# A two-layer hybrid backbone on one core: the scheduler's assumed delays between engines and for transfers raised, and its order and priorities chosen anew under them

## The chip, the cores and the metric

The kernel runs on one core of a Trainium2 chip. Time is device time in microseconds (us) of one execution, and the number that counts is the median of the runs: 2003.44 us of three (1996.93, 2003.58 and 2003.44). The core has TensorE for matmuls (PE, with its weight loads shown as PEld), VectorE (DVE), ScalarE (ACT), GpSimd (POOL) and SyncE (SP), which issues most transfers.

## What is computed

Two layers over 1024 latent tokens and 256 context tokens of width 1024. Each layer normalises and modulates its input, projects it once (34 tiles of 128 columns and 16 small gate columns), runs three groups of heads on the pieces, projects the concatenated outputs back and adds them to the stream through a gate. Cut to what matters:

```python
for l in range(DEPTH):                                   # 2 layers
    mod = jax.nn.silu(c) @ w_mod[l] + b_mod[l]           # shift, scale, gate; the same for the context
    h  = rms_norm(x, norm_g[l]) * (1.0 + scale) + shift
    hc = rms_norm(y, norm_g[l]) * (1.0 + scale_c) + shift_c
    pl, pc = split_cols(h @ w_in[l]), split_cols(hc @ w_in[l])
    a_l, a_c = attention_mixer(...)   # windowed attention, 8 heads, rotary, sink, context keys; * silu(z)
    g_l, g_c = gdn_mixer(...)         # gated DeltaNet, both directions: conv, l2norm, chunks of 128 here,
                                      # a triangular inverse per chunk, then a chain over the chunks
    r_l, r_c = lru_mixer(...)         # conv, block-diagonal gates, linear scan in both directions
    x = x + gate * (concat(a_l, g_l, r_l) @ w_out[l])
    y = y + gate_c * (concat(a_c, g_c, r_c) @ w_out[l])  # layer 0 only
return rms_norm(x, final_g)
```

## The kernel before

The kernel has no loop that fixes the order of its instructions. Each piece of work is a Python generator (a thread) that yields operations with an engine, a cost and the buffers that are read and written: `inproj` multiplies the input projection's tiles, `kq_thread`, `v_thread` and `lru_thread` do the convolutions and gates, `prep_thread` and `inv_thread` prepare the DeltaNet chunks, `gjob`, `gside` and `gchain` run them, `att_block`, `att_half` and `score_thread` do the attention, `stage3` splits the outputs (`osplit`) and multiplies the output projection, `mod_thread` makes the modulation vectors. Large products are done in three fp32r passes (high half times high half, high times low, low times high), which the rows show as `whi` and `wlo`.

While the program is built, `Driver.run` plays a list scheduler. It keeps a planned clock for every engine and every buffer; at each step it takes, of all threads that stand ready, the one with the lowest key, that is the planned start plus the thread's priority (`PR` for layer 0, `PR1` for layer 1) plus a few penalties, and issues its instruction. What it issues becomes the fixed order of the engine's queue on the chip; the planned times themselves reach the chip in no form. The delays that it assumes:

- `LATS` (line 22): what is added after the end of an operation on PE, ACT, DVE or POOL before another engine may use the result.
- the line `end = self.dma + ...` (line 394): what is added after a transfer's planned end, and `dmabw`, the bytes per microsecond that transfers share.
- `Driver.fill` (called in `run`): where PE's next operation would start later than PE is free by its plan, and it opens a fresh PSUM buffer, the scheduler issues dummy matmuls of the identity with itself (128x128 fp32, 0.226 us each by its plan) until 0.3 us before that start; a filler is put in only where at least two fit. In the orders below these are the rows `psum<-ident_114 128x128`. Before the first real products, `warm` issues more of the same kind. A filler is an instruction like any other: it runs whether PE had to wait there or not.

PE's order is thus work, and fillers where the plan has a hole. Lines that the steps below speak of: 595 is the helper that issues every matmul; 705 and 711 are ACT's copy and PE's transposes for the modulation; 741 and 747 the sums of squares before a norm; 1256 and 1263 take a projection's PSUM away; 1554 is the transfer that crosses two halves of the partitions for the LRU gates; 1728 to 1781 are the copies of a DeltaNet chunk's inverse; 1888 and 1894 finish DeltaNet; 1968, 1989, 2056, 2088 and 2090 are attention's maximum, exponential, transposes and their copies; 2023 transposes its denominators. The attention's keys and queries (`kstd`, `qstd`) are loaded through ACT's own DMA queue (`q_att = "aq"`), the rest through SP's.

Of the kernel before, what the change touches and what calls it, by code (L numbers as in the profile page):

```python
# [18 lines left out]
EPS = 1e-6  # L19
XSIZE, YSIZE = 21376, 21584  # L20
LAT = 0.2
LATS = dict(pe=0.2, act=0.14, dve=0.12, pool=0.08)
HOST = dict(gq="pool", aq="act")
BLK = {"A": (256, 512), "B": (768, 512), "C": (0, 256)}
SPANS = ((0, 512), (512, 512), (1024, 258))
# [208 lines left out]
class Driver:  # L234


    def __init__(self):
        self.eng = dict(pe=0.0, act=0.0, dve=0.0, pool=0.0, sp=0.0, aq=0.0, gq=0.0)
        self.dma = 0.0
        self.threads, self.blocked = [], []  # L240
        self.set, self.free = "", ("inproj", "oproj", "mod0")
        self.trace = None
        self.regions = []
        self.clock = Clock()
        self.PR = {"att": -2.23, "att_k": -6.13, "att_q": -24.94, "atth": 0.51, "ba": 1.24, "evac": -0.21,
                   "gchain": 0.84, "gdn_q": -4.1, "gdn_v": 0.22, "gfin": -5.94, "gprep": 0.61, "gside": 1.08,
                   "inproj": 1.35, "inv": 0.4, "lru_x": -0.17, "lru_z": -1.8, "modlate": -1.43, "modload":
                   -12.04, "norm": 0.21, "normA": -13.11, "normB": -12.92, "normC": -5.67, "nrmB": -2.77,
                   "nrmC": 0.25, "oproj": 0.39, "osplit": -1.28, "prep": -3.38, "ptev": -5.63, "resid": -0.56,
                   "rope": 1.5, "score": -0.16, "warm": 4.18, "wprep": -10.67, "z": -1.27}  # L250
        self.ops, self.late = [], False
        self.PR1 = {"att": -1.75, "att_k": -24.84, "att_q": -1.75, "atth": -0.51, "ba": 0.55, "evac": 0.23,
                    "gchain": 1.03, "gdn_q": -5.85, "gdn_v": 0.65, "gfin": 2.81, "gprep": -1.81, "gside": 0.09,
                    "inproj": 0.71, "inv": 0.22, "lru_x": -0.54, "lru_z": 1.01, "normA": -0.05, "normB": 2.27,
                    "normC": 13.57, "oproj": -0.41, "osplit": 0.31, "prep": -2.79, "ptev": -6.8, "resid":
                    -11.31, "rope": 6.72, "score": -2.09, "wprep": 0.18, "z": -1.15}
        self.margin, self.setpen, self.tilepen = 2.88, 1.24, 0.43
        self.cap = {"pe": 0.51, "dve": 0.34, "act": 0.28, "pool": 0.53}
        self.filler, self.fillmin = None, 2
        self.port, self.tile, self.sync, self.dry = dict(dve=0.0, pool=0.0), "", {}, False  # L260
        self.waitc, self.dmabw = dict(act=0.06, dve=0.05, pool=0.04, sp=0.047, gq=0.04), 300e3

    def spawn(self, gen, prio=0.0, name="", done=None):
        th = Thread()
# [40 lines left out]
    def ready(self, name, R, Wr):  # L305

        start = self.eng[name]
        lat = LATS.get(name, 0.0)
        for b in R:
# [17 lines left out]
    def run(self):  # L327
        while self.threads or self.blocked:
            self.settle()
            best = None  # L330
            for th in self.threads:
                _, cost, fn, R, Wr = th.op
                name, st = th.eng, th.st
                start = self.ready(name, R, Wr)
                p = th.prio

                if name in self.cap and start > self.eng[name] and p < -self.cap[name]:
                    p = -self.cap[name]
                key = start + p
                if name == "pe" and start > self.eng["pe"] and not th.free:  # L340
                    key += self.margin
                if name == "pe":
                    if st != self.tile:
                        key += self.tilepen
                elif st and st not in self.set.split(","):
                    key += self.setpen
                if best is None or key < best[0]:
                    best = (key, start, th)
            if best is None:
                if not self.blocked:  # L350
                    break
                raise RuntimeError("stuck: " + "; ".join(f"{t.name}:{t.op[0]}:{getattr(t.op[1], 'name', '')}" for t in self.blocked))
            _, start, th = best
            self.threads.remove(th)
            _, cost, fn, R, Wr = th.op
            name, st = th.eng, th.st
            if name == "pe":
                if self.filler:
                    self.fill(start, Wr)
                if st != self.tile:  # L360
                    start += 0.093
                    self.tile = st
            elif st and st not in self.set.split(","):
                start += 1.3
                self.set = {"t": "t,e", "l": "l,e", "s": "s", "e": "t,e"}[st]
                if st == "l":

                    self.table("natural_log_exp_and_others")
            if self.trace is not None:
                self.trace(th.name, name, start, cost, R, Wr)  # L370
            if not self.dry:
                fn()
            pre = set()
            k = len(self.ops)
            for b in R:
                pre.add(b.wo)
            for b in Wr:
                if not b.dram:
                    pre.add(b.wo)
                    pre.update(b.ro.values())  # L380

            seen = {}
            for i in pre:
                if 0 <= i < k and self.ops[i] != name and i > self.sync.get((name, self.ops[i]), -1):
                    seen[self.ops[i]] = max(i, seen.get(self.ops[i], -1))
            for e2, i in seen.items():
                self.sync[name, e2] = i
            start += self.waitc.get(name, 0.0) * max(0, len(seen) - 1)
            if name in ("sp", "aq", "gq"):
                self.eng[name] = start + (0.6 if name == "gq" else 0.42)  # L390
                if name in HOST:
                    self.eng[HOST[name]] = self.eng[name]
                self.dma = max(self.dma, start) + cost / self.dmabw
                end = self.dma + (4.5 if name == "gq" else 2.2)
            else:
                end = start + cost if name != "pe" else self.clock.run(start, cost, 0.5 if st else 1.0)
                self.eng[name] = end
                if name in ("dve", "pool") and not any(b.psum for b in R) and not any(b.psum for b in Wr):
                    self.port["pool" if name == "dve" else "dve"] = end
                end += LATS[name]  # L400
            for b in R:
                b.ro[name] = k
            for b in Wr:
                b.wo, b.ro = k, {}
            self.ops.append(name)
            for b in R:
                if end > b.r:
                    b.r, b.re = end, "" if name in ("sp", "gq") else name
            for b in Wr:
                b.virgin = False  # L410
                if end > b.w:
                    b.w, b.we = end, "" if name in ("sp", "gq") else name
            self.advance(th)
# [142 lines left out]
class Build:  # L556
# [467 lines left out]
    def params(self):  # L1024
# [37 lines left out]
        for k in "aeflr":  # L1062
            for l in range(2):
                yield ops[k, l]

    ORDER = ("gdn_k0", "gdn_q1", "gdn_v1", "gdn_k1", "gdn_q0", "gdn_k2", "gdn_q2", "lru_x3", "att_q0", "gdn_z3",
             "gdn_k3", "lru_x0", "lru_z3", "att_v0", "gdn_q3", "gdn_v3", "lru_z0", "lru_x2", "lru_x1", "lru_z2",
             "att_q2", "gdn_v0", "att_z2", "lru_z1", "gdn_z2", "gdn_v2", "att_q3", "att_q1", "att_k0", "gdn_z1",
             "gdn_z0", "att_z3", "att_z0", "att_z1")
    ORDER1 = ("gdn_q0", "lru_z2", "gdn_q1", "gdn_k0", "gdn_k1", "gdn_v3", "gdn_k2", "gdn_k3", "gdn_q2",  # L1070
              "gdn_v2", "gdn_q3", "lru_x3", "lru_z1", "lru_x1", "gdn_z0", "att_v0", "lru_z0", "lru_x2",
              "lru_z3", "att_z1", "gdn_v1", "att_q2", "gdn_v0", "lru_x0", "att_k0", "att_q0", "att_q3",
              "att_q1", "att_z0", "att_z2", "att_z3", "gdn_z2", "gdn_z3", "gdn_z1")

    def ev(self, *k):
        return self.events.setdefault(k, Event())
# [13 lines left out]
    def phase_a(self, l):  # L1090
# [10 lines left out]
        C["lock_lru"], C["lock_kq"], C["lock_att"], C["lock_inv"] = self.lock(1), self.lock(2), self.lock(2), self.lock(1)  # L1101
        order = self.order(l, self.ORDER1 if l else self.ORDER)
        jobs, boxes = self.wjobs(l, order)
# [1229 lines left out]
```

## Time and profile before

| | |
|---|---|
| median of the runs | 2003.44 us |
| the profiled execution's own time | 2003.42 us |
| its span, first to last instruction | 2001.7 us |
| PE busy | 1936.9 us, 97% |
| DVE, ACT, POOL busy | 1312.9, 1062.0, 424.1 us (66%, 53%, 21%) |
| mean granted clock of TensorE | 0.986 |
| moved by DMA | 338.04 MB, 169 GB/s over the span |

The profiled execution and the median agree within 0.02 us, so sums are made against either; 1.7 us lie outside the span. PE is busy nearly all the time, so what can be won or lost lies in three places: time in which PE waits, time in which its clock is granted at the lower of its two levels, and matmuls that compute nothing (the fillers). A profile's busy time of PE has the fillers in it. The program runs through these stretches: 0 to 110 us loads and first norms, 110 to 545 the input projection of layer 0 with convolutions and gates, 545 to 1000 DeltaNet, attention and the start of the output projection, 1000 to 1110 the turn to layer 1, 1110 to 1530 its input projection, 1530 to 1870 its DeltaNet and attention, then the last projection, and a tail of 11.7 us without matmuls.

### The profile page before, as it was taken

How to read it: one execution, taken by the hardware profiler on the slowest of the kernel's cores; microseconds unless marked ns; L12 is line 12 of the kernel's file. 1: busy time of each engine (PE TensorE's matmuls, PEld its weight loads, DVE VectorE, ACT ScalarE, POOL GpSimd, SP SyncE). 2: the span in 40 equal slices, each digit the busy share in tenths (PEclk: the TensorE clock that was granted, in tenths of full speed). 3: DMA queues.
4: the chain of work that ended last, by engine and by line, in shares of the span. 5: the costliest groups of instructions: out<-in, count | busy, mean ns of one | idle time of the engine just before them, and what ended most of it. 6: DMA issues, size and time to landing. Idle time of an engine off the chain costs nothing. (4 is left out here: it accounts for less than half of the span.)

```text
span 2001.7 us, 35422 instructions
## 1 busy us (share of the span) xinstructions
PE 1936.9 (97%) x13244; PEld 1560.5 (78%) x13244; DVE 1312.9 (66%) x2568; ACT 1062.0 (53%) x1897; POOL 424.1 (21%) x604
## 2 busy tenths in 40 slices
PE   8999999999999989999999999999999999999997
PEld 5688778888888966767788788877777888776786
DVE  5666699697844465774624668899788434787433
ACT  4467677565533254665523577676665322566432
POOL 2302100100055631001332111200001765100232
PEclk9999999999999999999999999999999999999998
DMA  8135633614588897655633156562444878544653
GB/s 301 35 108 172 180 110 95 182 54 137 182 280 266 263 299 239 201 163 148 225 106 119 45 170 177 156 166 64 137 142 173 284 224 258 162 133 124 200 169 105
DMA packets 311597, 338.04 MB, mean 169 GB/s; under 512 B 62993, under 2 KB 220289, under 8 KB 311425
## 3 DMA queue, kind: packets, MB, share of 16 engines
q1 hardware_dynamic: 290544, 321.05, 52.0%
q10 hardware_dynamic: 20880, 14.73, 2.4%
q8 instruction: 104, 1.70, 0.4%
q14 instruction: 69, 0.56, 0.1%
HBM read 235.58 MB, written 94.87 MB: 165 GB/s over the span
## 5 line engine op out<-in xcount | busy, mean ns | idle before, releaser
L595 PE MATMUL psum<-regx,whi 128*128 128x512 f32 (+1 forms) x3328 | 952.1, 372 | 8.5 <-ACT regy L1263 3.7
L595 PEld LDWEIGHTS psum<-regx,whi 128*128 128x128 f32 x3328 | 592.2, 189 | 125.8 <-issue 12.2
L595 PE MATMUL psum<-regx,wlo 128*128 128x512 f32 (+1 forms) x1664 | 609.8, 366 | 0.0
L595 PEld LDWEIGHTS psum<-regx,wlo 128*128 128x128 f32 x1664 | 314.6, 189 | 52.9 <-DVE wlo L876 0.2
L595 PE MATMUL psum<-regy,regy 128*128 128x128 f32 (+4 forms) x4064 | 318.7, 265 | 10.4 <-DMA regy<-regy 4.2
L595 PEld LDWEIGHTS psum<-regy,regy 128*128 128x128 f32 (+2 forms) x4064 | 266.1, 148 | 55.1 <-issue 26.9
L871 ACT ACTIVATE whi<-raw 128x1024 fp32r<-128x1024 f32 (+1 forms) x132 | 125.6, 952 | 167.7 <-PE psum L595 144.7
L595 PE MATMUL psum<-regx,regx 128*64 128x256 f32 (+2 forms) x1184 | 190.3, 363 | 4.7 <-DMA regx<-kstd 2.5
L595 PEld LDWEIGHTS psum<-regx,regx 128*64 128x64 f32 (+1 forms) x1184 | 112.9, 162 | 56.3 <-issue 25.9
L595 PE MATMUL psum<-regy,whi 128*128 128x512 f32 (+1 forms) x576 | 156.4, 359 | 0.1
L876 DVE TENSOR_TENSOR wlo<-raw,whi 128x1024 fp32r<-128x1024 f32 (+1 forms) x100 | 114.2, 1143 | 54.6 <-ACT whi L871 54.3
L876 POOL TENSOR_TENSOR wlo<-raw,whi 128x768 fp32r<-128x768 f32 x32 | 60.8, 1899 | 388.0 <-ACT whi L871 385.1
L1989 ACT ACTIVATE regx<-regx,regx 128x640 f32<-128x640 f32 (+2 forms) x144 | 109.0, 760 | 21.0 <-DVE regx L1981 11.9
L1356 DVE SCALAR_TENSOR_TENSOR regy<-regy,gcv,regy 128x1282 f32<-128x1282 f32 x72 | 111.9, 1556 | 9.3 <-ACT regy L1352 7.9
L595 PEld LDWEIGHTS psum<-regy,whi 128*128 128x128 f32 x576 | 101.4, 189 | 19.7 <-issue 4.2
L1263 ACT ACTIVATE regy<-psum 128x512 f32<-128x512 f32 (+1 forms) x124 | 65.2, 527 | 93.8 <-PE psum L595 87.4
L1669 POOL TENSOR_TENSOR regy<-regy,regy 128x512 f32<-128x512 f32 x76 | 96.8, 1295 | 75.9 <-DMA regy<-kqd 49.3
L1712 POOL TENSOR_SCALAR_AFFINE_SELECT regy<-regy 128x128 f32<-128x128 f32 (+1 forms) x240 | 68.8, 323 | 207.7 <-DMA regy<-Md 77.8
L2199 DVE SCALAR_TENSOR_TENSOR regy<-psum,modT,regy 128x512 f32<-128x512 f32 (+1 forms) x40 | 27.8, 696 | 126.9 <-PE psum L595 126.9
L2090 ACT ACTIVATE regx<-psum 128x512 f32<-128x512 f32 x114 | 65.2, 593 | 81.6 <-PE psum L2056 77.1
L595 PE MATMUL psum<-regy,wlo 128*128 128x512 f32 (+1 forms) x288 | 102.7, 357 | 0.3 <-POOL wlo L876 0.2
L2056 PE MATMUL psum<-ident,regx 128*128 128x128 f32 x640 | 94.0, 279 | 4.8 <-ACT regx L2090 1.9
(200 smaller groups left out, 2606.8 us busy)
## 6 DMA issues: line engine op xcount, KB each, us to landing
raw<-in_win_dram SPq DMA_DIRECT2D x68, 512.0 KB
raw<-in_wout_dram SPq DMA_DIRECT2D x64, 384.0 KB
regy<-kqd SPq DMA_DIRECT2D x76, 256.0 KB
raw<-in_wmod_dram SPq DMA_DIRECT2D x32, 512.0 KB
regy<-od SPq DMA_DIRECT2D x24, 512.0 KB
regy<-egd SPq DMA_DIRECT2D x40, 256.0 KB
regy<-ktd SPq DMA_DIRECT2D x40, 256.0 KB
regy<-vtd SPq DMA_DIRECT2D x40, 256.0 KB
```

What stands on the lines that cost most here:

```text
L595: self.nc.tensor.matmul(out, lhsT, rhs, start=start, stop=stop, skip_group_check=True)
L871: yield ("act", c_act(n), lambda: nc.scalar.activation(hi.t[:, :n], raw.t[:, :n], AF.Copy), [raw], [hi])
L876: (nc.gpsimd if e == "pool" else nc.vector).tensor_tensor(lo.t[:, :n], raw.t[:, :n], hi.t[:, :n].bitcast(F32), OP.subtract)
L1263: yield ("act", c_act(n), lambda: nc.scalar.activation(dst.t[:m, o:o + n], ps.t[:m, :n], AF.Copy), [ps], [dst])
L1356: yield ("dve", c_dve(GW), lambda: nc.vector.scalar_tensor_tensor(y.t[:, :GW], xp.t[:, k:k + GW], w[:, k:k + 1], y.t[:, :GW], OP.mult, OP. ...
L1669: yield ("pool", c_pool(512), lambda: nc.gpsimd.tensor_tensor(b.t, b.t, ga.t, OP.mult), [ga, b], [b])
L1712: nc.gpsimd.affine_select(out[:, :, 32 * b:32 * b + 32], src, [[0, 4], [0, 32]], OP.is_ge, 0.0, base=32 * b + 31 if up else -32 * b, chann ...
L1989: yield ("act:e", c_act(nk, 1) + .1, lambda: nc.scalar.activation(P, P, AF.Exp, bias=one(0, h), scale=-1.0, accum_out=one(8, h)), [Ps[j], ...
L2056: nc.tensor.transpose(pt.t[:, 128 * j:128 * j + 128], Ps[j].t[:, 128 * i:128 * i + 128], self.I.t)
L2090: yield ("act", c_act(512), lambda: nc.scalar.activation(PT.t, pt.t, AF.Copy), [pt], [PT])
L2199: yield ("dve", c_dve(n), lambda: nc.vector.scalar_tensor_tensor(xn.t[:, :n], ps.t[:, :n], g.t[:, 16 + dt, who:who + 1], xn.t[:, :n], OP.m ...
```

## The change

The assumed delays are raised, the transfers' bandwidth is lowered a little, all planned clocks start at 3 to 4 us instead of zero, and under these numbers priorities, tile orders, penalties and caps were chosen anew. No operation of the kernel's computation is added or removed; the order of nearly all of them moves, and the number of fillers with it.

```diff
-LATS = dict(pe=0.2, act=0.14, dve=0.12, pool=0.08)
+LATS = dict(pe=0.35, act=0.4, dve=0.4, pool=0.4)
...
-        self.eng = dict(pe=0.0, act=0.0, dve=0.0, pool=0.0, sp=0.0, aq=0.0, gq=0.0)
-        self.dma = 0.0
+        self.eng = dict(pe=4.0, act=4.0, dve=4.0, pool=4.0, sp=3.0, aq=4.0, gq=4.0)
+        self.dma = 4.0
...
-        self.PR = {"att": -2.23, "att_k": -6.13, "att_q": -24.94, "atth": 0.51, "ba": 1.24, "evac": -0.21,
+        self.PR = {"att": -2.03, "att_k": -10.38, "att_q": -23.44, "atth": 0.38, "ba": -2.37, "evac": 0.28,
...
-        self.margin, self.setpen, self.tilepen = 2.88, 1.24, 0.43
-        self.cap = {"pe": 0.51, "dve": 0.34, "act": 0.28, "pool": 0.53}
+        self.margin, self.setpen, self.tilepen = 2.91, 1.5, 0.43
+        self.cap = {"pe": 0.45, "dve": 0.35, "act": 0.03, "pool": 0.45}
...
-        self.waitc, self.dmabw = dict(act=0.06, dve=0.05, pool=0.04, sp=0.047, gq=0.04), 300e3
+        self.waitc, self.dmabw = dict(act=0.06, dve=0.05, pool=0.04, sp=0.047, gq=0.04), 285e3
...
-                end = self.dma + (4.5 if name == "gq" else 2.2)
+                end = self.dma + (5.0 if name == "gq" else 3.2)
...
-    ORDER = ("gdn_k0", "gdn_q1", "gdn_v1", "gdn_k1", "gdn_q0", "gdn_k2", "gdn_q2", "lru_x3", "att_q0", "gdn_z3",
+    ORDER = ("gdn_k2", "gdn_q1", "gdn_k0", "gdn_v3", "gdn_k1", "gdn_q0", "gdn_v0", "lru_x3", "att_q2", "gdn_z3",
...
```

Counted over PE's whole order, the matmuls go from 10335 to 10453, and all of the difference is fillers: 139 before, 257 now. Of these, 106 and 110 stand among the first loads and norms, before the input projection runs without a break; behind that there are 33 in 7 places before (2, 5, 2, 2, 9, 5, 8) and 147 in 21 places now (2, 19, 3, 4, 24, 3, 2, 3, 6, 15, 3, 11, 6, 4, 4, 7, 2, 7, 6, 3, 13). What stands around DeltaNet changes too. Of the 400 32x32 matmuls with which layer 0 starts its chunks' inverses, 360 stood ahead of attention's first transposes and 80 do now; in layer 1 it was all 400, now 160. Of the input projection, 264 matmuls stood between the first of these 32x32 rows and the end of attention in layer 0, and 24 do now (150 and 84 in layer 1).

Three places in PE's order. The first is the first late modulation chunk of layer 0, whose transposes (L711) need ACT's copy of a product of PE. Before, `regy` rows are DeltaNet, L1894 finishes two of its chunks:

```order
L1894 MATMUL psum_87<-ident_114,regy_4437 128x128 x4
L595 MATMUL psum_81<-regy_4413,regy_4419 64x64 x4
L595 MATMUL psum_85<-regy_4232,regy_4422 64x64 x4
L595 MATMUL psum_84<-ident_114 128x128 x2
L1894 MATMUL psum_84<-ident_114,regy_4438 128x128 x4
L595 MATMUL psum_82<-regy_4411,regy_4420 32x32 x8
L595 MATMUL psum_82<-regy_4414,regy_4425 32x32 x8
L711 MATMUL psum_86<-ident_114,regx_6082 128x128 x4
```

Now the same transposes stand behind attention's scores (`regx,regx`, 256 columns each), and two fillers:

```order
L595 MATMUL psum_82<-regx_4936,regx_4939 128x256
L595 MATMUL psum_82<-regx_4937,regx_4939 128x256
L595 MATMUL psum_82<-regx_4936,regx_4939 128x256
L595 MATMUL psum_82<-regx_4937,regx_4939 128x256
L595 MATMUL psum_87<-regx_4934,regx_4939 128x256
L595 MATMUL psum_87<-regx_4935,regx_4939 128x256
L595 MATMUL psum_86<-ident_114 128x128 x2
L711 MATMUL psum_86<-ident_114,regx_5051 128x128 x4
```

The small 32x32 products just ahead of the transposes are replaced by longer ones that depend on loads alone.

The second place is the end of attention in layer 0. Before, output projection rows (`regy,whi` and `regy,wlo`) stand between the last products with the values (64x256) and the last denominators (L2023):

```order
L595 MATMUL psum_84<-regx_6080,regx_6046 64x256 x2
L595 MATMUL psum_84<-regx_6077,regx_6046 64x256 x2
L595 MATMUL psum_83<-regx_6079,regx_6046 64x256 x2
L595 MATMUL psum_83<-regx_6076,regx_6046 64x256 x2
L595 MATMUL psum_81<-regy_7190,whi_172 128x512
L595 MATMUL psum_81<-regy_7183,whi_172 128x512
L595 MATMUL psum_81<-regy_7190,wlo_174 128x512
L595 MATMUL psum_81<-regy_7190,whi_172 128x512
L595 MATMUL psum_81<-regy_7183,whi_172 128x512
L595 MATMUL psum_81<-regy_7190,wlo_174 128x512
L2023 MATMUL psum_82<-ident_114,regx_6086 8x128
```

Now fillers stand there:

```order
L2056 MATMUL psum_80<-ident_114,regx_5034 128x128
L2056 MATMUL psum_80<-ident_114,regx_5035 128x128
L595 MATMUL psum_82<-regx_5046,regx_4938 64x256 x2
L595 MATMUL psum_82<-regx_5049,regx_4938 64x256 x2
L595 MATMUL psum_81<-ident_114 128x128 x24
L2023 MATMUL psum_81<-ident_114,regx_5056 8x128
L595 MATMUL psum_80<-ident_114 128x128 x3
L2056 MATMUL psum_80<-ident_114,regx_5037 128x128
```

The output projection of layer 0 no longer begins before the last attention block is transposed (90 of its matmuls stood ahead of that, none does now).

The third place is the end of PE's order: the last output projection, fillers, and the sum of squares of the final norm (`ones`). Before:

```order
L595 MATMUL psum_82<-regx_15910,whi_172 128x512
L595 MATMUL psum_82<-regx_15909,wlo_174 128x512
L595 MATMUL psum_86<-ident_114 128x128 x8
L595 MATMUL psum_86<-regy_15427,ones_119 128x512
```

Now:

```order
L595 MATMUL psum_84<-regx_16035,whi_172 128x512
L595 MATMUL psum_84<-regx_16034,wlo_174 128x512
L595 MATMUL psum_80<-ident_114 128x128 x13
L595 MATMUL psum_80<-regy_15516,ones_119 128x512
```

Five more fillers stand between the same two operations.

## Rows read from the trace of the kernel before

**Rows 1.** The page: busy time of each engine, share of the span, instructions

```profile
PE 1936.9 (97%) x13244; PEld 1560.5 (78%) x13244; DVE 1312.9 (66%) x2568; ACT 1062.0 (53%) x1897; POOL 424.1 (21%) x604
```

**Rows 2.** Stretches of the run: length, busy time (instructions) by engine, clock, DMA

```profile
core 0: us, PE busy (x) PEld busy (x) DVE busy (x) ACT busy (x) POOL busy (x), PEclk, DMA share, GB/s
0.00:110.00 110.00, 98.26 (x594) 70.79 (x595) 68.28 (x124) 52.65 (x93) 31.00 (x40) 0.97 0.45 153
110.00:1990.00 1880.00, 1838.65 (x12652) 1489.69 (x12650) 1238.17 (x2439) 1006.18 (x1800) 388.48 (x561) 0.99 0.56 170
1000.00:1110.00 110.00, 108.99 (x604) 90.34 (x602) 44.44 (x68) 31.86 (x51) 29.87 (x25) 1.00 0.32 105
1870.00:1990.00 120.00, 119.55 (x523) 96.68 (x521) 43.25 (x49) 40.46 (x53) 36.04 (x22) 1.00 0.51 156
```

**Rows 3.** PE's waits from 110 to 1990 us: total us, times, longest

```profile
PE psum L711 <- ACT regx L705: 4.4, 2, 2.3
PE psum L595 <- DMA regy<-regy: 4.2, 2, 3.4
PE psum L595 <- ACT regy L1263: 3.7, 3, 2.9
PE psum L595 <- POOL regy L1781: 3.0, 2, 2.5
...
PE psum L595 <- DMA regx<-kstd: 2.5, 2, 1.5
PE psum L595 <- DVE regx L1256: 2.3, 1, 2.3
PE psum L2056 <- ACT regx L2090: 1.9, 1, 1.9
PE psum L595 <- DVE regy L741: 1.7, 2, 1.2
PE psum L595 <- DVE regy L809: 1.5, 1, 1.5
PE psum L1894 <- DVE regx L2088: 1.4, 1, 1.4
...
PE psum L595 <- DMA regx<-qstd: 1.4, 1, 1.4
...
PE psum L1894 <- DVE regy L1888: 1.1, 1, 1.1
...
PE psum L595 <- DVE wlo L876: 0.2, 1, 0.2
```

**Rows 4.** Two of the seven stretches with the lower clock, columns as in rows 2

```profile
224.00:234.00 10.00, 8.02 (x34) 4.82 (x35) 5.67 (x13) 4.03 (x6) 0.21 (x2) 0.66 0.63 178
...
1706.00:1716.00 10.00, 8.94 (x57) 8.60 (x58) 6.41 (x24) 0.76 (x2) 3.50 (x3) 0.66 0.83 242
```

**Rows 5.** Timeline of PE: start, length, instructions, and the wait before them

```profile
29.04 7.53 PE L595 MATMUL psum<-ident 128*128 128x128 f32 x66
...
711.47 1.11 PE L711 MATMUL psum<-ident,regx 128*128 128x128 f32 x4 [2.34 <-ACT regx L705]
...
1718.29 2.61 PE L595 MATMUL psum<-regx,regx 128*128 128x256 f32 x16 [1.37 <-DMA regx<-qstd]
```

**Rows 6.** Timeline of ACT's queue: issues of the attention's loads

```profile
705.88 3.28 ACTq L600 DMA_DIRECT2D regx<-kstd  x4
...
1709.45 0.38 ACTq L600 DMA_DIRECT2D regx<-qstd  x1
```

**Rows 7.** Timeline of the end, DVE and PE

```profile
1986.50 1.95 PE L595 MATMUL psum<-ident 128*128 128x128 f32 x16
...
1988.15 0.69 DVE L741 TENSOR_TENSOR regy<-regy,regy 128x512 f32<-128x512 f32 x1 [0.69 <-ACT regy L747]
1988.89 1.13 PE L595 MATMUL psum<-regy,ones 128*128 128x512 f32 x2 [0.45 <-DVE regy L741]
```

More of the change, by code (lines that the diff above doesn't have):

```diff
@@ L244, in __init__ @@
         self.clock = Clock()
-        self.PR = {"att": -2.23, "att_k": -6.13, "att_q": -24.94, "atth": 0.51, "ba": 1.24, "evac": -0.21,
[L246 to L250, printed above, removed]
@@ L251, in __init__ @@
-        self.ops, self.late = [], False
[L252 to L256, printed above, removed]
@@ L257, in __init__ @@
-        self.margin, self.setpen, self.tilepen = 2.88, 1.24, 0.43
-        self.cap = {"pe": 0.51, "dve": 0.34, "act": 0.28, "pool": 0.53}
+        self.PR = {"att": -2.03, "att_k": -10.38, "att_q": -23.44, "atth": 0.38, "ba": -2.37, "evac": 0.28,
+                   "gchain": 0.14, "gdn_q": -7.53, "gdn_v": 1.15, "gfin": -2.6, "gprep": 0.05, "gside": 0.87,
+                   "inproj": 1.32, "inv": 0.3, "lru_x": -0.17, "lru_z": -1.78, "modlate": -1.51, "modload":
+                   -18.36, "norm": 0.86, "normA": -14.03, "normB": -20.5, "normC": -14.47, "nrmB": -4.95,
+                   "nrmC": 0.93, "oproj": -2.68, "osplit": -2.43, "prep": -4.88, "ptev": -2.64, "resid": 0.29,
+                   "rope": 3.63, "score": -0.16, "warm": 5.4, "wprep": -8.27, "z": -1.59}
@@ new lines, in __init__ @@
+        self.ops, self.late = [], False
+        self.PR1 = {"att": -2.89, "att_k": -27.69, "att_q": -0.58, "atth": -0.73, "ba": -3.03, "evac": 0.4,
+                    "gchain": -4.34, "gdn_q": -7.45, "gdn_v": 0.76, "gfin": 2.56, "gprep": -1.98, "gside": -0.5,
+                    "inproj": 0.76, "inv": 0.22, "lru_x": -0.54, "lru_z": -2.86, "normA": 0.93, "normB": 2.36,
+                    "normC": 8.47, "oproj": 0.35, "osplit": -0.41, "prep": -2.77, "ptev": -8.75, "resid": -8.03,
+                    "rope": 11.72, "score": -1.25, "wprep": -1.6, "z": -1.47}
@@ L1064, in params @@
                 yield ops[k, l]
-    ORDER = ("gdn_k0", "gdn_q1", "gdn_v1", "gdn_k1", "gdn_q0", "gdn_k2", "gdn_q2", "lru_x3", "att_q0", "gdn_z3",
[L1067 to L1073, printed above, removed]
+    ORDER = ("gdn_k2", "gdn_q1", "gdn_k0", "gdn_v3", "gdn_k1", "gdn_q0", "gdn_v0", "lru_x3", "att_q2", "gdn_z3",
+             "att_v0", "lru_x0", "lru_z3", "gdn_k3", "gdn_q2", "gdn_q3", "gdn_z0", "lru_z0", "att_z1", "gdn_v1",
+             "lru_z2", "lru_x2", "att_q3", "gdn_z1", "lru_z1", "gdn_v2", "att_q0", "att_k0", "lru_x1", "att_z2",
+             "att_z3", "att_q1", "att_z0", "gdn_z2")
+    ORDER1 = ("gdn_q0", "lru_z3", "gdn_q1", "gdn_k0", "gdn_k1", "gdn_v2", "gdn_k3", "gdn_k2", "gdn_q2",
+              "gdn_v3", "gdn_q3", "lru_x0", "lru_z2", "lru_x1", "gdn_z2", "lru_z1", "lru_z0", "lru_x3",
+              "att_v0", "att_z2", "gdn_v1", "gdn_v0", "lru_x2", "att_q0", "att_k0", "att_q1", "att_q2",
+              "att_q3", "gdn_z1", "gdn_z0", "att_z3", "gdn_z3", "att_z1", "att_z0")
     def ev(self, *k):
```

## The prediction

> **What bounds the kernel now.** I read the page first: PE is busy for 1936.9 of 2001.7 us and no other engine is near it, the next being DVE with 1312.9 [rows 1]. So the order of PE's queue is the time, and all that a new order can change is what PE does besides its work. The table of stretches gives this in three parts. Up to 110 us PE idles 110 - 98.26 = 11.7 us; there the first loads set the pace, and both orders issue the same loads first. From 110 to 1990 us it idles 1880 - 1838.65 = 41.35 us, and its granted clock is 0.99 there, so about 0.01 x 1880 = 18.8 us of full-speed time are lost at the lower level [rows 2]. Behind 1990 us lie 11.7 us in which the last norm runs on other engines.
>
> The list of PE's waits tells what the 41.35 us are: 41 waits in 27 rows, of which the twelve with waits over 1 us and the last are shown, and no large one. Thirteen waits are longer than 1 us: 2.3 and 2.1 for ACT's copy before L711, 3.4 for the LRU transfer, 2.9 for L1263, 2.5 for POOL, 2.3, 1.9, 1.5, 1.5, 1.4, 1.4, 1.2 and 1.1 [rows 3]; the 2.1 is what the first row's 4.4 leaves. They sum to 25.5 us, and the other 28 to 15.85. The lower clock follows the longer ones: seven times the granted clock falls to 1.2 GHz, each time around one of these waits. Two of the seven are shown, 34% of 10 us each, so 3.4 us lost each [rows 4]; two more lose as much and three some 1.7 us.
>
> The third part is not a wait. A filler costs what work costs: 66 records, two to a filler, take 7.53 us, so 33 fillers take 7.53 and one takes 0.228 us [rows 5]. The 33 late fillers of before are 7.5 us. So between 110 and 1990 us some 41.35 + 18.8 + 7.5 = 67.6 us are not work, and only these can move.
>
> **The change, part by part.** *Work.* Nothing is added or removed but fillers, so PE's products cost what they cost now.
>
> *Fillers.* Behind the first stretch they go from 33 to 147, that is 114 x 0.228 = 26.0 us more on the engine that sets the end. Nothing hides them. They are no loss where PE would have waited as long anyway, and a loss elsewhere; I count them in full and count waits apart. Ahead of 110 us they go from 106 to 110; PE waits there for loads, so the four are taken at nothing (0.9 us if the loads were early).
>
> *Waits that become shorter.* The plan now allows 0.35 to 0.4 us after an operation where it allowed 0.08 to 0.2, some 0.25 us more, and 1.0 us more after a transfer. The planned distance between an operation and the one that needs it thus grows by 1 us where one transfer or four operations lie between, which is about what most waits have behind them (a product of PE, an ACT or DVE copy, a second vector operation, PE again). Where there is no work to put in between there are fillers, and the wait is gone too. I therefore take 1 us from every wait. The 28 short ones vanish, 15.85 us; of the thirteen long ones 25.5 - 13 = 12.5 us stay. Bounds: none is shortened (0 us) and all vanish (41.35 us); I take the value between, since the places shown bear it out. At the first modulation transposes PE waited 2.34 us [rows 5] behind two rows of small 32x32 products; now six score products and two fillers stand ahead of them.
>
> *The clock.* It falls around waits that last; if thirteen long waits shrink to half (25.5 to 12.5), I take half of the 18.8 us as won back, 9.4. Bounds are 0 and 18.8, and fillers, which are products, speak for the upper half.
>
> *The places that lose.* At the end of the kernel 8 fillers and then 0.45 us of waiting covered the chain resid, square, add [rows 7]. Two more fillers would have been enough; five are added, 0.7 us too many. DVE's add ends at 1988.84 and PE starts at 1988.89 [rows 7], so a hand-over takes 0.05 us where the plan now has 0.4: the new delays are longer than the chip's. At the end of attention in layer 0, 24 + 3 fillers stand where the output projection stood, 6.2 us; PE's wait there before was 1.9 us, for L2090 [rows 3]. From 1000 to 1110 and from 1870 to 1990 us PE idled 1.0 and 0.45 us [rows 2], and 15 + 3 + 11 fillers now stand at the turn to layer 1, 3 + 6 between output tiles of layer 0 and 6 + 3 between those of layer 1. These are all in the 26.0 us.
>
> *DeltaNet beside attention.* Before, most chunks' inverses ran ahead of attention, with the input projection's tail between them; now most stand between attention's rows. It changes what waits on what, but the sum of work per engine is the same, and DVE and ACT are busy for 66% and 53% [rows 1]; I take it at nothing, with 10 us to either side for the range, about a quarter of the 41.35 us.
>
> *Sum.* 2003.4 + 26.0 - 15.85 - 13.0 - 9.4 = 1991.2 us against the profiled execution's 2003.4, which is also the median. **Forecast: 1991 us.** A simpler form of the sum tells where it turns: with R for the waits and lost clock that remain, now 60.2 us, the time is 2003.4 + 26.0 - 60.2 + R = 1969.2 + R. The change breaks even at R = 34; I expect 22.
>
> **A rule that speaks against it.** The rows first: the attention's second query load was issued on ACT's queue at 1709.45 us [rows 6] and PE was released at 1718.29 [rows 5], 8.8 us later, for 512 KB. The Trainium skill's page "DMA: Bandwidth & Descriptors", section "Anatomy of one DMA — SWDGE (gpsimd) path", gives, for GpSimd's path, a fixed 2.0 us and bytes over 436e3 per us for one transfer, an estimate of 3.2 us for this size; the old 2.2 us and the shared bandwidth would then have been enough, and longer ones only buy fillers. By it what the sum takes from the five waits on transfers in rows 3 (1 us each, 0.8 for the shorter of the LRU's) would not be had from the new delays, and the sum would be 4.8 us higher, 1996. The trace does not agree with it at this place: the load took nearly three times as long, so I keep the 1 us.
>
> **The rivals.**
>
> *Fillers without waits (slower).* The long waits may have other causes than the assumed delays. ACT's queue was held 3.28 us by the issue of four key loads at 705.88 [rows 6], and the copy that L711 waited for 2.34 us came behind them; the plan charges 0.42 us an issue, before and now. If the thirteen long waits and the clock stay and only the 28 short ones go, the time is 2003.4 + 26.0 - 15.85 = 2013.6, and with two or three new holes at the changed seam of attention and output projection (1.9 us there before) up to 2013.6 + 3 x 1.9 = 2019. It decides from R = 44 on. For it: hand-overs of 0.05 us, the places that lose, and waits on queues that no delay models. Against it: nearly all late waits would have to stay at their size although every order around them is new.
>
> *They cancel (no change).* Half of the 60.2 us goes: 2003.4 + 26.0 - 30.1 = 1999.3. For it: an order with three times the fillers has by its own account fewer operations ready to choose from.
>
> *All covered.* Every wait behind 110 us goes and with it the clock's falls: 1969.2; with a tenth left, 1975. For it: from 110 us to the end of layer 0's input projection there is not one filler even under the long delays. Against it: transfers can be late by more than 1 us, as the 8.8 us show.
>
> *The change does not do what it says.* Only the order reaches the chip, and it moves nearly everywhere; this is excluded.
>
> **How the numbers follow.** The forecast and what lies around it, R from 14 to 34: 0.46, with its middle just on the side of faster. All covered, R under 14: 0.14. They cancel, R from 34 to 44: 0.21. Slower, over 44: 0.19. What the measurement can tell from no change is about 0.5%, 10 us: faster means under 1993.4, which is R under 24; that takes the 0.14 and 0.34 of the 0.46. Same, 1993.4 to 2013.4, has 0.12 and 0.21, slower 0.19. For 8 in 10 the range leaves out a part of the first and of the last: 1974 (R = 5) to 2018 (R = 49). The forecast's own range is 1983 to 2003.
>
> **What would show it.** In the profile after, the group of `psum<-ident` must have 514 records and some 26 us more of PE's time. Idle time from 110 us on should be near 12.5 us, the granted clock there near 0.995, and the waits for L705, L1263 and POOL at L1781 short or gone. The forecast is wrong if waits over 2 us stand in the new places, at the end of attention in layer 0 above all, or if attention beside DeltaNet has more waits than the 41 of before; then R is over 34. It is also wrong, to the good side, if the clock is granted in full from 110 us on.

## The result: slower, and the profile after

Median of the changed kernel 2019.99 us (2011.73 to 2023.15), of the kernel before 2001.74 us beside it; the ratio is 1.0086 with a 95% interval of 1.0061 to 1.0111. A second measurement of the same pair gave 1.0102 (1.0079 to 1.0126). The forecast was 1991 us, faster; the time lies above the upper end of the range, 2018.

The profiled execution below is the shortest of its set, 2011.73 us (span 2010.0); where a typical one (e12 below, span 2020.9 us) differs, it is said. First the busy line and the stretches, columns as in [rows 1] and [rows 2]:

```profile
PE 1950.5 (97%) x13480; PEld 1584.1 (79%) x13480; DVE 1327.6 (66%) x2568; ACT 1058.0 (53%) x1892; POOL 421.6 (21%) x604
```

```profile
0.00:110.00 110.00, 101.68 (x614) 73.28 (x615) 72.90 (x125) 54.16 (x95) 31.61 (x40) 0.98 0.45 157
110.00:1990.00 1880.00, 1840.52 (x12827) 1504.18 (x12819) 1246.22 (x2436) 1000.02 (x1792) 385.34 (x561) 0.99 0.55 169
```

From 110 to 1990 us PE idles 1880 - 1840.52 = 39.5 us, against 41.35 before [rows 2], and its clock is again 0.99. The new order has 114 more fillers there and hardly less waiting; in the typical execution it idles 46.4 us there, 5.1 more than before. PE's waits in that stretch (total us, times, longest), the largest six and the last:

```profile
PE psum L595 <- ACT regy L1762: 8.6, 2, 6.5
PE psum L595 <- ACT regy L1263: 8.2, 4, 4.0
PE psum L595 <- ACT regy L2128: 5.8, 2, 4.9
PE psum L595 <- DVE regy L809: 2.0, 2, 1.3
PE psum L595 <- DMA regx<-kstd: 2.0, 2, 1.3
PE psum L595 <- DVE regy L2129: 2.0, 4, 0.8
...
PE psum L2056 <- ACT regx L1989: 0.2, 1, 0.2
```

Against [rows 3] the list of this execution has changed its owners, hardly its size. L705, the LRU transfer and POOL at L1781 are gone, as forecast. Three waits longer than any before stand in their place, each behind ACT: 6.5 us for L1762 (a copy of DeltaNet's inverse), 4.9 for L2128 (the split of an input of the output projection), 4.0 for L1263 (a projection's PSUM). The clock falls in five places instead of seven, and around these waits; two are shown:

```profile
920.00:930.00 10.00, 5.03 (x12) 2.98 (x12) 3.05 (x3) 2.20 (x3) 1.57 (x1) 0.66 0.92 266
...
1626.00:1636.00 10.00, 3.50 (x36) 3.25 (x37) 1.56 (x2) 2.73 (x6) 4.14 (x4) 0.62 1.03 367
```

The second is also one in which all DMA engines are busy (share 1.03, 367 GB/s): the attention's keys and queries of layer 1 are being loaded. The timeline of that place, ACT's queue, ACT and PE:

```profile
1624.15 0.37 ACTq L600 DMA_DIRECT2D regx<-qstd  x1
1624.56 7.08 ACTq L600 DMA_DIRECT2D regx<-kstd  x4
1633.10 0.63 ACT L1762 ACTIVATE regy<-psum 64x256 f32<-64x256 f32 x2
1633.52 0.80 PE L595 MATMUL psum<-regy 64*64 64x64 f32 x5 [6.50 <-ACT regy L1762]
```

ACT cannot do its next copy while its queue stands at the four key loads: 7.08 us here, 3.28 before in layer 0 [rows 6]. That row merges the four issues, which take 0.33 to 0.73 us each. In the chain of work that ended last, the third of them starts only when the query load issued ahead of them has landed:

```profile
1624.15 6.66 DMA regx<-qstd
...
1630.83 0.33 ACTq L600
```

So most of the 7.08 us is a wait for a transfer. The end of attention in layer 0, PE and ACT:

```profile
901.41 5.62 PE L595 MATMUL psum<-ident 128*128 128x128 f32 x48
...
918.88 0.27 PE L2023 MATMUL psum<-ident,regx 128*8 128x128 f32 x1
...
922.94 1.06 ACT L2128 ACTIVATE regy<-regy 128x1024 fp32r<-128x1024 f32 x1 [3.09 <-DMA regy<-od]
...
924.05 0.80 PE L595 MATMUL psum<-regy,whi 128*128 128x512 f32 x1 [4.90 <-ACT regy L2128]
```

24 fillers, and still, 12 us behind them, a wait of 4.90 us for the split, for whose input ACT had itself waited 3.09 us. PE was busy for 60.00 of the 60 us from 880 to 940 us in the order before, and for 51.55 now. At L1263, too, ACT had waited, 6.45 us for PE at a weight split (L871) ahead of the copy in its queue. So behind each of the three long waits stands a wait of ACT's own.

A sum of two profiled executions says where the time went: 118 more fillers at 0.228 us, +26.9; idle time over the whole span 2001.7 - 1936.9 = 64.8 before and 2010.0 - 1950.5 = 59.5 after, -5.3; PE's busy time without fillers 1936.9 - 139 x 0.228 = 1905.2 and 1950.5 - 257 x 0.228 = 1891.9, -13.3. Together +8.3, which is 2011.7. The same sum for the typical execution is +26.9, +3.9 (idle time 2020.9 - 1952.2 = 68.7) and -11.6 (1952.2 - 257 x 0.228 = 1893.6), together +19.2, near the difference of the medians, 18.3. The shortest execution thus shows the same work and fillers, but 9.2 us less of idle time than a typical one.

### The profile page after: what moved, and what is told of

Its sections match the earlier page's. It is cut to its first block, busy times and chain, and to the rows that moved or that the text cites. A ratio compares the mean times of both kernels' runs of the same rounds, so it can differ in the third digit from the quotient of the medians.

```text
span 2010.0 us, 35860 instructions
## 1 busy us (share of the span) xinstructions
PE 1950.5 (97%) x13480; PEld 1584.1 (79%) x13480; DVE 1327.6 (66%) x2568; ACT 1058.0 (53%) x1892; POOL 421.6 (21%) x604
## 4 chain that ended last, share of the span: by engine, by line
PE 81%; DVE 7%; DMA 6%; ACT 2%; issue 2%; SPq 0%; POOL 0%; ACTq 0%; DVEq 0%; POOLq 0%
PE psum L595 76%; PE psum L2056 3%; DMA regx<-rd 1%; PE psum L1238 1%; DVE regy L784 1%; DMA raw<-in_wmod_dram 1%; DMA regx<-kstd 1%; DMA raw<-in_win_dram 1%; DVE regy L605 1%; DVE regy L809 0%; DMA regy<-in_wmod_dram 0%; SPq L600 0%; DVE regy L1518 0%; DMA regy<-od 0%; DMA regy<-ktd 0%
## 5 line engine op out<-in xcount | busy, mean ns | idle before, releaser
L595 PEld LDWEIGHTS psum<-regx,whi 128*128 128x128 f32 x3328 | 593.5, 189 | 130.7 <-issue 18.4
L871 ACT ACTIVATE whi<-raw 128x1024 fp32r<-128x1024 f32 (+1 forms) x132 | 125.8, 953 | 193.1 <-PE psum L595 165.0
L595 PE MATMUL psum<-regx,regx 128*64 128x256 f32 (+2 forms) x1184 | 199.0, 365 | 3.6 <-DMA regx<-kstd 2.0
L1263 ACT ACTIVATE regy<-psum 128x512 f32<-128x512 f32 (+1 forms) x124 | 65.1, 527 | 119.1 <-PE psum L595 108.4
L1457 POOL TENSOR_SCALAR_AFFINE_SELECT regy<-regy 128x512 f32<-128x512 f32 (+1 forms) x48 | 30.9, 648 | 332.7 <-ACT regy L1452 331.0
```

What stands on the lines that cost most here:

```text
L595: self.nc.tensor.matmul(out, lhsT, rhs, start=start, stop=stop, skip_group_check=True)
L871: yield ("act", c_act(n), lambda: nc.scalar.activation(hi.t[:, :n], raw.t[:, :n], AF.Copy), [raw], [hi])
L1263: yield ("act", c_act(n), lambda: nc.scalar.activation(dst.t[:m, o:o + n], ps.t[:m, :n], AF.Copy), [ps], [dst])
L1457: yield ("pool", c_pool1(n), lambda: nc.gpsimd.affine_select(m3, s3, [[0, nch], [-1, 128]], OP.is_gt, 0.0, base=0, channel_multiplier=1), ...
```

## The experiments

Three theories were set against each other first. A: the fillers cost their 26 us. B: fillers stand where PE would wait anyway and are free; the new order has larger holes. C: of these holes, those at attention's loads come from ACT's queue, which the loads hold.

**Fillers left out, both kernels.** Planned clocks and order stay as they are; only the late fillers are not issued.

```diff
-            if not self.dry:
+            if not self.dry and t < 119.0:
                 self.filler(b)
```

> The changed order with its 147 late fillers left out; the 110 among the first loads and norms stay, and the order of all work on every engine is that of the changed kernel. Theory A (a filler costs its full 0.228 us because the plan's delays are longer than the chip's): 2020 - 33.5 = 1987 us, less what waits appear in their place, at most a third of it: 1987 to 1998. Theory B (fillers stand where PE has to wait anyway, so they cost nothing and keep the clock up): 2015 to 2030, with PE's idle time about 33 us longer than the 48 us of the changed kernel.

Measured: 2025.27 us, ratio 1.0124 (1.0102 to 1.0147), no faster than the changed kernel with them. The stretch from 110 to 1990 us:

```profile
110.00:1990.00 1880.00, 1809.49 (x12513) 1469.38 (x12513) 1240.81 (x2430) 995.78 (x1787) 380.50 (x558) 0.98 0.55 169
```

70.5 us of idle time instead of 39.5 (46.4 in the typical execution): the 33.5 us of fillers turned into 24 to 31 us of waits, and the granted clock went from 0.99 to 0.98. Theory A fell.

> The order of before without its 33 late fillers, all else as before. Theory A: 33 x 0.228 = 7.5 us less, 1994 us. Theory B: within 3 us of 2002, with idle time 7 us longer, or slower by a few us where the clock falls more often.

Measured: 1999.27 us, 1.0006 (0.9992 to 1.0019). The 33 fillers of before are free too. With no late fillers in either kernel, the two orders stand 1.2% apart (1.0124 against 1.0006).

**Attention's loads on SP's queue.** PE's order stays the same; the scheduler is not told.

```diff
-        eng = {"sp": self.nc.sync, "aq": self.nc.scalar, "gq": self.nc.gpsimd}[q]
+        eng = {"sp": self.nc.sync, "aq": self.nc.sync, "gq": self.nc.gpsimd}[q]
```

> The changed kernel with the attention's loads of keys and queries issued on SP's queue instead of ACT's, at the same places of the program. Theory C (ACT's queue, held by these issues for 3.1 us in layer 0 and 7.1 us in layer 1, makes PE's waits for L1762 of 2.1 and 6.5 us, the two largest of DeltaNet's inverses): both waits go below 0.5 us and with them one fall of the clock each, 8 to 14 us less: 2006 to 2012. Rival D (the wait moves to SP, whose queue then holds the loads of DeltaNet, so PE waits for those instead): within 5 us of 2020.

Measured: 2010.92 us, 1.0054 (1.0036 to 1.0073). The wait for L1762 is 2.4 us, once, in the place of 8.6:

```profile
PE psum L595 <- ACT regy L1762: 2.4, 1, 2.4
```

Against the kernel before as it is, the loss goes from 0.86 or 1.02% to 0.54%. Whether that is a part of what the change lost depends on what the same edit gives the order of before, which is the next run.

> Before with the same loads on SP's queue. Theory C: the waits for ACT's copy before L711 (2.3 and 2.1 us) shrink where ACT was held for 3.3 us, 2 to 6 us less: 1996 to 2000. Rival D: 2002 to 2010.

Measured: 1991.41 us, 0.9967 (0.9949 to 0.9985). The same one-line edit makes the kernel before faster, by 7 us, more than the 2 to 6 of theory C; it is the best version of this study. A wait of 3.2 us for L705 stays, so where the gain comes from is open. With the loads on SP's queue in both kernels the two orders stand 0.9% apart (1.0054 against 0.9967), as they did with the loads on ACT's. So the queue of these loads costs both orders about alike, and is at most a small part of what the change lost (0.15% by these ratios).

**The two halves of the change, each alone.** e5 is the kernel before with only `LATS`, the start clocks, `dmabw` and the transfers' delays of the change; e6 is the changed kernel with these five set back:

```diff
-LATS = dict(pe=0.2, act=0.14, dve=0.12, pool=0.08)
+LATS = dict(pe=0.35, act=0.4, dve=0.4, pool=0.4)
...
-                end = self.dma + (4.5 if name == "gq" else 2.2)
+                end = self.dma + (5.0 if name == "gq" else 3.2)
```

> The kernel before with its own priorities and tile orders, and only the assumed delays of the change (LATS, the delay and bandwidth of transfers, the clocks' start). The order now has 376 late fillers in 36 places instead of 33 in 7, among them 76 in one place within the input projection of layer 0, where PE did not wait before, and 58 near the end of attention in layer 1. It tells whether the delays or the newly chosen tables lose the time. Theory D (the delays alone do it: they are longer than the chip's, so the scheduler keeps PE from work that was ready): well above the changed kernel, 2030 us or more, a ratio to the kernel before of 1.015 or more. Theory T (the tables do it; delays by themselves only exchange waits for fillers): within 0.5% of the kernel before, 1992 to 2012 us.

Measured: 2137.6 us, 1.0693 (1.0665 to 1.0722).

> The changed kernel's priorities, tile orders, penalties and caps under the old assumed delays. The order has 150 late fillers in 23 places, and 18 matmuls of the output projection ahead of the end of attention in layer 0 (90 before, none in the changed kernel). Theory T (the tables lose the time, by the order of DeltaNet, attention and output projection that they give): as slow as the changed kernel, 2010 to 2025 us, with waits over 2 us at the end of attention in layer 0. Theory D (the long delays lose it): back at the kernel before, 1995 to 2005. Both tables and delays were chosen for each other, so a time above the changed kernel's would speak for neither part alone but for the pairing.

Measured: 2097.69 us, 1.0496 (1.0463 to 1.0528). Both alone are far worse than the pair. The row with the longest wait of e5, and under it of e6:

```profile
PE psum L595 <- DVE regy L1269: 11.6, 2, 9.9
```

```profile
PE psum L595 <- DVE regy L1269: 12.9, 1, 12.9
```

By its number e5 meets theory D, but then e6 should have come back to the kernel before, and it did not. So neither "the delays" nor "the tables" can be charged with the loss from these two: here each table of priorities worked only with the delays it was chosen under, and each of the two mixtures is a new order with a wait of 10 to 13 us.

**The delays in the order before.** To judge the delays without a new order, e9 keeps the order of before, written down as a list of 7133 thread numbers (`SEQ`), and runs only the planned clocks with the new delays. What changes is where the scheduler sees holes, and fills them.

```diff
-            for th in self.threads:
+            for th in [t for t in self.threads if t.idx == SEQ[len(self.ops)]]:
```

> The kernel before with its own order of operations written down and kept, and only the planned clocks run with the assumed delays of the change, so that the scheduler puts fillers where these delays see a hole. There are 463 late fillers in 77 places (33 in 7 before, 147 in 21 in the changed kernel); nothing else moves but which PSUM buffer an operation takes. At 0.228 us each the 430 more are 98 us. Theory L (the assumed delays are far longer than the chip's: most of these holes do not exist, PE would have had its operands): most of the fillers cost what they take, 2060 us or more, a ratio of 1.03 or more. Theory F (fillers stand where PE waits anyway, as the two runs without fillers suggested): within 1% of before.

Measured: 2057.24 us, 1.0282 (1.0254 to 1.031). 56.7 of the 98 us of additional fillers are paid.

```profile
110.00:1990.00 1880.00, 1857.08 (x13232) 1530.10 (x13232) 1232.31 (x2425) 995.91 (x1785) 371.92 (x553) 1.00 0.55 167
```

Idle time falls by 18.4 us, to 22.9, and the granted clock there is 1.00 for 0.99; the two together pay for nearly all of the other 41. Theory L holds, a little under its number: more than half of the holes that the new delays see in a good order are not there on the chip, and a scheduler that plans with them gives up that order (e5).

**The end of attention in layer 0.** In e7 the output projection of layer 0 waits for all of attention; in e10 its splits wait for seven of the eight blocks. Edits, in that order:

```diff
-            yield from self.until((l, "osp", "A", 1))
+            yield from self.until((l, "osp", "A", 1), *[(0, "att", k) for k in range(8) if l == 0])
...
-                    yield from self.until(*need[i // 2])
+                    yield from self.until(*need[i // 2], *[(0, "att", k) for k in range(7) if l == 0])
```

> The kernel before, in which the output projection of layer 0 may begin only when all eight attention blocks of that layer are done; nothing else is changed, and its order behind that place is nearly the one of before. 90 matmuls that stood between attention's last rows go behind them, as in the changed kernel, and 25 more fillers (2 and 16 at that place, 7 later) are planned in. Theory S (the lost cover at this seam is a main cause: the changed kernel shows 18.5 us of waits, fillers and lost clock there where the kernel before shows none): slower than before by 9 to 18 us, 1.0045 to 1.009. Theory N (the seam's holes are the slack of the rest, PE would stand later anyway): within 3 us of before.

Measured: 2003.18 us, 1.0018 (1.0003 to 1.0033). It is 3.5 us slower than the kernel before beside it, just over the 3 of theory N. Theory S fell in this form: without the cover, PE waits at the seam for 0.6 us and runs 36 more fillers' records.

> The kernel before, in which in layer 0 not the output projection but already the splits of its inputs (L2125 to L2129) may begin only when seven of the eight attention blocks are done, as in the changed kernel, where their buffers come free only when both DeltaNet chains have ended, late beside attention. 24 fillers are planned at the seam. Delaying the projection alone cost 0.18%. If the rest of what the changed kernel shows at the seam (a wait of 4.9 us for the split at L2128, 18.5 us of waits, fillers and lost clock in all) comes from the splits being late, this run shows waits for L2128 behind attention and a ratio of 1.005 to 1.009. If not, it stays at 1.002.

Measured: 2014.35 us, 1.0077 (1.0053 to 1.0102). PE's waits from 890 to 940 us in e10, and under them in the changed kernel:

```profile
PE psum L595 <- ACT regy L2128: 3.8, 2, 2.3
PE psum L595 <- DVE regy L2129: 2.0, 3, 0.8
```

```profile
PE psum L595 <- ACT regy L2128: 5.8, 2, 4.9
PE psum L595 <- DVE regy L2129: 2.0, 4, 0.8
...
```

The same two rows. What costs time in e10 is less that matmuls of the projection no longer stand between attention's rows (e7), it is more that their inputs (stored, loaded back, split on ACT, then on DVE) become ready only afterwards, piece by piece, while PE waits for each.

**Told to the scheduler.** e8 is the kernel before with the loads on SP's queue, and the scheduler books them there:

```diff
-HOST = dict(gq="pool", aq="act")
+HOST = dict(gq="pool", aq="sp")
```

> The kernel before with attention's loads of keys and queries issued on SP's queue, and with the scheduler told so (it no longer books the issue on ACT). The plan changes with it: 68 fillers where the same edit without telling it has 33. If what the queue change gave (1991.4 against 1998.5 us) is the freed ACT queue, this has it too, 1988 to 1995 us; if the good order of before is what matters, and any new plan under unchanged tables loses some, it lies between, 1995 to 2010 us.

Measured: 2007.05 us, 1.0039 (1.0023 to 1.0055), 0.7% slower than e4, which has the same queues and the old order. Here a truer plan under unchanged tables gave a worse order.

**Which loads.** e11 moves only the eight key loads of the changed kernel.

```diff
-        eng = {"sp": self.nc.sync, "aq": self.nc.scalar, "gq": self.nc.gpsimd}[q]
+        eng = {"sp": self.nc.sync, "aq": self.nc.sync if nbytes == 655360 else self.nc.scalar, "gq": self.nc.gpsimd}[q]
```

> The changed kernel with only attention's eight key loads issued on SP's queue; its query loads stay on ACT's. PE's order is the same. If ACT was held in issuing the key loads (3.08 and 7.08 us, behind a query load on the same queue), nearly all that moving keys and queries together gave comes from this: the wait of 6.50 us for ACT at L1762 in layer 1 is gone or under 2 us, and the ratio to before is 1.004 to 1.007. If the query loads matter too (16 issues beside attention's exponentials), it stays above 1.007.

Measured: 2024.9 us, 1.0118 (1.0096 to 1.014): nothing won. Its largest waits, and the row for L1762:

```profile
PE psum L595 <- DMA regx<-qstd: 9.7, 3, 4.7
PE psum L595 <- ACT regy L1263: 9.1, 4, 4.0
...
PE psum L595 <- ACT regy L1762: 1.9, 1, 1.9
```

The wait for L1762 went from 9.9 us (the changed kernel, measured again, below) to 1.9, and three waits of 9.7 us in all for the query loads took its place (one of 3.7 there). So C was half right: ACT's queue is held, but freeing it is worth something only when the query loads come in time too, which they did when keys and queries shared one queue on SP (e3).

> The changed kernel itself, unchanged, beside the runs above on the same chip, for direct comparison: 1.0061 to 1.0111 by the first measurement, 2012 to 2022 us.

Measured: 2019.98 us, 1.0102 (1.0079 to 1.0126). Its profile is a typical execution, and shows what the shortest one above lacks:

```profile
PE psum L595 <- ACT regy L1762: 9.9, 2, 6.8
PE psum L595 <- ACT regy L1263: 9.1, 4, 4.0
PE psum L595 <- ACT regy L2128: 5.1, 2, 4.7
PE psum L595 <- DMA regx<-qstd: 3.7, 1, 3.7
PE psum L595 <- DMA raw<-in_wmod_dram: 2.8, 4, 1.8
```

The second query load of layer 0 came 3.75 us too late here, and not at all too late in the shortest execution. The stretch from 110 to 1990 us of this execution, with 46.4 us of idle time:

```profile
110.00:1990.00 1880.00, 1833.58 (x12793) 1497.19 (x12792) 1238.42 (x2434) 996.97 (x1788) 380.94 (x558) 0.99 0.56 169
```

## Why the prediction was wrong

**The step that failed is "waits that become shorter".** It took 1 us from every wait, on the ground that the plan now allows more between an operation and its user: 28 short waits gone (-15.85), the thirteen long ones down from 25.5 to 12.5 us. Measured on the same split: eight waits longer than 1 us sum to 23.4 us (6.5, 4.9, 4.0, 2.1, 1.9 and three of 1.3), and 28 short ones, with what no row lists, to 16.1. The booked -28.85 became -1.9, and +5.1 in the typical execution. The reasoning held each wait in its place and made it shorter, while the order around it was new throughout. A new order has its own waits, and the thing to estimate was the quality of that order, for which e5, e6 and e8 show how easily it is lost.

**The fillers** were counted right (514 records) and priced wrongly in kind. The sum booked 26.0 us in full and the waits apart. Leaving them out (e1) makes 24 to 31 us of waits for 33.5 of fillers and lowers the clock, so fillers and waits are nearly one term, PE's holes: before 41.35 + 7.5 = 48.9 us, after 39.5 + 33.5 = 73. The prediction had that equivalence in a half sentence ("no loss where PE would have waited as long anyway") and did not use it. Read so, an order with 147 late fillers says by itself that its plan has 33.5 us of holes, some 26 more than before. Where a plan's holes are mostly not real, fillers cost time: in e9 58% of their length.

**The clock**: -9.4 was booked, and the grant is still 0.99. The places at 1.2 GHz are fewer (five for seven) and longer, as the long waits are.

**Work "costs what it costs now"**: without fillers it took 13.3 us less of PE's busy time, and 11.6 in the typical execution. This was in no step, and goes in the other direction than the loss. A part of it is the clock: in the two falls shown PE is busy for 5.03 and 3.50 of 10 us, in those of before for 8.02 and 8.94 [rows 4], so less of its work runs at the lower level. Nor is all the rest the order's: over the executions kept here the same difference gives 1890.6 to 1904.8 us in the changed order (with e1, e3, e11, e12) and 1895.4 to 1905.8 in that of before (with e2, e4). Less what the lower level costs while PE is busy, an estimate from the granted clock in each trace, they are 1874.7 to 1878.2 and 1880.8 to 1887.2, so some 7 us are the order's. What shortens them is open, since the ends of matmuls are modelled and can hide waits. The form 1969.2 + R gives 2027.5 with the R found (39.5 + 18.8), 16 us too much, and these 13.3 and 3.4 us less idling in the first 110 us, less 0.9 for four more fillers there, are the difference.

**The places that lose** were named, and the end of attention in layer 0, with a wait of 4.9 us, is one of the three that show long waits. The prediction gave the seam 6.2 us of fillers and thought of three holes of 1.9 us at most. Its reason was also a step short: the lost cover alone is worth 0.18% (e7), with the late splits 0.77% (e10). DeltaNet beside attention, taken at nothing, has the largest row, 8.6 us for L1762. At the tail 0.7 us too many fillers were expected: DVE's add ends at 1996.81 and PE starts at 1997.32, some 0.5 us, which counts for nothing beside this.

**The rival "fillers without waits"** (2013.6 to 2019) came nearest, with its condition R over 44 met (58.3), but that its number fits is luck. It charged the fillers in full, kept the old long waits and let the short ones go; measured, the fillers are free in this order (e1), the long waits are new ones, the short ones stay, and PE's work is shorter. Of its named reason, the key loads on ACT's queue, e3 bears out that they make the wait for L1762, and e4 that the order of before pays about as much for that queue (0.33% against 0.32 to 0.48%). The 3.28 us of [rows 6] were in the profile before and were taken as a cause of one wait, not as something that a new order may meet at a worse moment.

**What is settled and what is not.** Shown: the fillers are not the loss (without them the orders stand 1.2% apart, e1 and e2), the queue of the attention's loads is hardly a part of it (0.9% apart without it, e3 and e4), the assumed delays exceed the chip's in a good order (e9), and late splits at the seam, put into the order of before, cost 0.77%, nearly the size of the whole (e10). Not shown is that the changed kernel loses its time there: it has the same two waits, but no run made its splits early. These do not add up one by one, since PE's work without fillers came out 12 to 13 us shorter in the new order. The waits for L1263, 8.2 us against 3.7 [rows 3], were read from the trace alone: at 1272.50 us ACT starts a weight split (L871) after a wait of 6.45 us for PE, then a table load and an activation, and the PSUM that PE needs is emptied behind them. No run took that away.

## What to carry to other kernels

These are rules from one kernel. Price a new schedule by its holes as a whole, fillers and waits together, and not by shortening the waits of the old one: where the order is new, the list of waits is new. Delays and priorities of this list scheduler proved one set, and neither could be judged, moved or undone alone; the one edit here that gained on both kernels left the order alone and moved transfers off the queue of an engine that computes. Where a projection's inputs come back through memory, what counted more at the seam was when those inputs are ready, and less what stands between whose matmuls.

## What the runs showed of the hardware

Issuing loads is not free for the engine that issues them. Four key loads held ACT for 3.08 us in layer 0 and 7.08 us in layer 1, with one query load issued just ahead of them on the same queue, while a single load took 0.37. In layer 1 most of that is no issuing: the third key load starts when the query load has landed, 6.66 us after its issue. From 1626 to 1636 us the DMA engines moved 367 GB/s at a busy share of 1.03. The Trainium skill's page "DMA: Bandwidth & Descriptors", section "Issuing engines are not separate DMA queues", says that transfers of all issuing engines run on the same 16 DMA engines, and that issuing from several saves only the time on the issuer's sequencer, usually small beside the transfer itself. e11 fits the first part, since the keys on another queue only moved the wait to the queries. A single issue, 0.37 us against 6.66 us to landing, agrees with the second; the 7.08 us in which ACT stood do not.

A load of 512 KB can be in use only 11 us after its issue: in the typical execution the second query load of layer 0 was issued at 627.06 us and PE, which had waited 3.75 us for it, started at 638.40. From 624 to 640 us the DMA engines moved 265 GB/s at a busy share of 0.85.

```profile
627.06 0.38 ACTq L600 DMA_DIRECT2D regx<-qstd  x1
```

```profile
638.40 1.22 PE L595 MATMUL psum<-regx,regx 128*128 128x256 f32 x8 [3.75 <-DMA regx<-qstd]
```

The prediction had read 8.8 us at another place of the kernel before [rows 5, 6] and kept that for a single case. Three such loads now show 6.66, 8.8 and 11.3 us, further apart than the 1.0 us by which the change raised the assumed delay of a transfer.
